# Eight routed experts on one core: ranking the experts, stacking a small expert's row parts, and splitting weights 2048 columns at a time

## The chip, the core and the metric

The kernel runs on one core of a Trainium2 chip. The metric is the device time of one execution in microseconds; a run gives the median over executions. The engines are TensorE (PE in the rows, its weight loads PEld), VectorE (DVE), ScalarE (ACT), GpSimd (POOL) and SyncE (SP), which here issues the DMA loads. They have queues of their own, work through them in order, and meet only at semaphores.

## The reference

All values are float32. The input is 256 tokens of width 1024. A first block of two layers mixes tokens and ends each layer with a feed-forward part. In the second layer this part is a mixture of eight experts:

```python
logits = (xt @ router)                       # 256 x 8
top_logit, top_e = lax.top_k(logits, 2)      # two experts for each token
gates = jax.nn.softmax(top_logit, axis=-1)
# each expert e, on the tokens that chose it (hidden width 3584):
yb = (jax.nn.silu(h @ w_gate[e]) * (h @ w_up[e])) @ w_down[e]
y = sum over a token's two experts of gate * yb
```

So 512 rows in all go to eight experts, and every expert's three matrices (1024 x 3584, 1024 x 3584 and 3584 x 1024) are read once. A second block of two layers follows, with attention, gating, a short convolution and a feed-forward part of width 2816.

## The kernel before

**Float32 in parts.** TensorE multiplies in a reduced form of float32. To keep the precision, `split` writes each operand as a high part H (a rounding copy on ScalarE, line 182) and a low part L = source - H (on VectorE, line 183). A product is three matmuls: H by H, L by H and H by L. For weights, `raw` (line 193) issues the load of 1 MB (128 partitions of 2048 columns) on SyncE into one of five buffers `wr`, and `parts` splits it in two halves of 1024 columns, into five buffers each of `wh` and `wl`.

**Routing.** `moe` computes logits, picks two experts per token by comparing all pairs, counts earlier tokens of the same expert with a triangular matmul, and so gives each row a slot `pos` in its expert. `one_hot` turns slots into a 0/1 matrix `oh`, with which TensorE gathers the rows of two experts at once, 128 slots each, into `xH` and `xL`. An expert with over 128 rows would set `over`, and `overflow` (a branch on that value ahead of the third expert) would work on the remaining rows.

**Experts.** They run one after the other in the order of their number, two to a gather. For each, a loop runs over seven blocks of 512 hidden columns. `gate_up` loads two 1 MB pieces each of the gate and up matrices, and multiplies the gathered rows (stationary, 128 x 128) with 512 weight columns (moving): 8 row blocks x 3 products x 2 matrices = 48 matmuls. ScalarE and VectorE make silu(gate) * up. `down`, always one block behind, transposes the result by four TensorE transposes (line 158), splits it into `aH` and `aL`, and adds 24 matmuls to the two output banks `py`. When an expert is done, its output is scaled by the gates (`y`), and `back` returns it to the tokens through the transposed one-hot `ohT` and adds it to `moe_out`.

**What sets the order.** The instructions are put in order by a planner when the program is built, by its own estimates of when each is ready; on each engine that order is then fixed. Loads are kept in the order of their use. Five early loads are placed in buffers that the stage uses only later (`places`), so that they can be issued ahead of the stage.

**After the experts.** The second block uses the same `wr`, `wh` and `wl` buffers through `cols`, `fm2` and `down`. In its feed-forward layer a 1 MB piece makes 48 matmuls of 256 columns, after which VectorE scales the result (line 1592) and does the short convolution (`conv3`, lines 1637 to 1639).

## Time and profile before

| | |
|---|---|
| median of 3 runs | 2883.36 us (2870.65 to 2900.98) |
| the profiled execution | 2886.99 us, of which the span 2885.2 us |
| granted TensorE clock, mean | 0.965 of full speed |
| TensorE / VectorE / ScalarE / GpSimd busy | 2750.6 / 1988.4 / 1468.3 / 348.5 us |
| loaded and stored by DMA | 585.8 MB, 203 GB/s over the span |
| loads of expert weights | 3 x 112 of 1024 KB |

The span is the time from the first to the last instruction. A busy share is a mean over stages that differ, so rows of single stages count for more. A row such as `L154 PE MATMUL psmoe<-wl,xH` names the line, the engine, the operation, and the tile written and the tiles read. Matmuls overlap in the array, so the time of one (some 0.40 us for 512 columns) is longer than the step from one to the next. An arrow in a row points to what the engine waited for. PEclk is the granted TensorE clock, DMA share the busy share of the 16 DMA engines.

### The profile page before, as it was taken

Reading aid. Unit: us, or ns where it says so; the run is one execution under the profiler, and the core shown is the slowest. Engines: PE = TensorE matmul, PEld = TensorE weight load, DVE = VectorE, ACT = ScalarE, POOL = GpSimd, SP = SyncE. Lnnn points to the kernel's source line nnn. Section 1 sums busy time; section 2 is a strip of 40 time slices with the busy share of each in tenths; the row PEclk is TensorE's granted clock in tenths of the full one; section 3 lists DMA queues with packets and bytes.
Section 4 is the critical chain, followed back from the end, with each engine's and each line's share of the span. In section 5 each row is a group of like instructions: output and inputs, shape, how many; then the busy total and the mean of one; then the engine's idle time right before and its main releaser. Section 6 shows DMA issues by size and latency. Waiting matters only on the chain. (4 is left out here: it accounts for less than half of the span.)

```text
span 2885.2 us, 42860 instructions
## 1 busy us (share of the span) xinstructions
PE 2750.6 (95%) x17006; PEld 2257.8 (78%) x17006; DVE 1988.4 (69%) x2753; ACT 1468.3 (51%) x2032; POOL 348.5 (12%) x256
## 2 busy tenths in 40 slices
PE   6998999999998879999989999999999999999999
PEld 4677656778886766677867777778777889998999
DVE  4685474322225796488878888888889868856784
ACT  3313243322224332477757777767777646644563
POOL 1420012211001610100000000000000221301120
PEclk9898799999999998999999999999999999999999
DMA  6122155333333224579988999899989835553453
GB/s 227 51 74 74 52 150 193 96 123 94 97 99 105 81 88 140 173 293 352 319 321 325 322 353 344 328 338 362 337 325 349 307 114 175 183 183 117 161 184 109
DMA packets 108098, 585.77 MB, mean 203 GB/s; under 512 B 12657, under 2 KB 19825, under 8 KB 54129
## 3 DMA queue, kind: packets, MB, share of 16 engines
q1 hardware_dynamic: 107888, 582.95, 57.5%
q8 instruction: 136, 2.23, 0.3%
q14 instruction: 74, 0.60, 0.1%
HBM read 580.80 MB, written 2.10 MB: 202 GB/s over the span
## 5 line engine op out<-in xcount | busy, mean ns | idle before, releaser
L183 DVE TENSOR_TENSOR wl<-wr,wh 128x1024 fp32r<-128x1024 f32 x978 | 1169.5, 1225 | 477.9 <-ACT wh L182 465.6
L182 ACT CAST wh<-wr 128x1024 fp32r<-128x1024 f32 x992 | 1003.8, 1044 | 681.1 <-PE psffn L154 193.2
L154 PE MATMUL psmoe<-wh,xH 128*128 128x512 f32 x896 | 354.9, 397 | 3.4 <-ACT wh L182 3.4
L154 PE MATMUL psmoe<-wl,xH 128*128 128x512 f32 x896 | 356.2, 398 | 1.0 <-DVE wl L183 0.7
L154 PE MATMUL psmoe<-wh,xL 128*128 128x512 f32 x896 | 355.5, 397 | 0.0
L154 PEld LDWEIGHTS psmoe<-wl,xH 128*128 128x128 f32 x896 | 168.3, 188 | 45.6 <-DVE wl L183 6.5
L154 PEld LDWEIGHTS psmoe<-wh,xH 128*128 128x128 f32 x896 | 168.4, 188 | 44.4 <-ACT wh L182 5.0
L154 PE MATMUL pssf<-oh,wl 128*128 128x256 f32 x704 | 199.5, 284 | 0.0
L154 PE MATMUL pssf<-ohT,wh 128*128 128x256 f32 x704 | 199.2, 284 | 0.0
L154 PEld LDWEIGHTS psmoe<-wh,xL 128*128 128x128 f32 x896 | 168.4, 188 | 39.1
L154 PE MATMUL pssf<-oh,wh 128*128 128x256 f32 x704 | 198.9, 284 | 0.0
L154 PE MATMUL psmoe<-wh,aL 128*128 128x512 f32 x448 | 178.3, 398 | 2.0 <-DVE aL L183 2.0
L154 PE MATMUL psmoe<-wh,aH 128*128 128x512 f32 x448 | 175.6, 397 | 2.5 <-ACT aH L182 2.5
L154 PE MATMUL psmoe<-wl,aH 128*128 128x512 f32 x448 | 163.3, 400 | 0.0
L1551 POOL TENSOR_SCALAR x<-x,fin 128x256 f32<-128x256 f32 x8 | 12.2, 1542 | 1057.5 <-DMA wr<-w_in 1057.3
L154 PE MATMUL psffn<-h2L,wh 128*128 128x512 f32 x352 | 138.7, 394 | 1.3 <-POOL h2L L257 1.3
L154 PE MATMUL psffn<-h2H,wh 128*128 128x512 f32 x352 | 138.2, 395 | 1.0 <-ACT h2H L256 1.0
L154 PE MATMUL psffn<-h2H,wl 128*128 128x512 f32 x352 | 137.5, 392 | 0.0
L154 PEld LDWEIGHTS pssf<-oh,wl 128*128 128x128 f32 x704 | 135.2, 192 | 0.0
L154 PEld LDWEIGHTS pssf<-ohT,wh 128*128 128x128 f32 x704 | 135.1, 192 | 0.0
L154 PEld LDWEIGHTS pssf<-oh,wh 128*128 128x128 f32 x704 | 135.0, 192 | 0.0
L154 PEld LDWEIGHTS psmoe<-wh,aL 128*128 128x128 f32 x448 | 84.2, 188 | 24.4 <-DVE aL L183 4.4
(476 smaller groups left out, 5624.6 us busy)
## 6 DMA issues: line engine op xcount, KB each, us to landing
wr<-moe_w_gate SPq DMA_DIRECT2D x112, 1024.0 KB, 7.0
wr<-moe_w_up SPq DMA_DIRECT2D x112, 1024.0 KB, 6.6
wr<-moe_w_down SPq DMA_DIRECT2D x112, 1024.0 KB, 7.0
wm<-mod_w SPq DMA_DIRECT2D x96, 512.0 KB, 4.3
wr<-f_up SPq DMA_DIRECT2D x44, 1024.0 KB, 4.9
wr<-w_in SPq DMA_DIRECT2D x52, 512.0 KB, 3.8
wr<-w_in SPq DMA_DIRECT2D x16, 1024.0 KB, 5.0
wr<-f_down SPq DMA_DIRECT2D x16, 1024.0 KB, 5.0
```

The costliest lines, as they stand in the source:

```text
L154: i = self.nc.tensor.matmul(out, lhsT, rhs, start=start, stop=stop, **kw)
L182: self.nc.scalar.copy(H, src)
L183: (eng or self.nc.vector).tensor_sub(L, src, H.bitcast(F32))
L1551: nc.gpsimd.tensor_scalar(x[:, k], x[:, k], fin[:, k:k + 1], None, op0=ALU.mult)
```

## The change

**Ranking.** VectorE counts the rows of each expert and ranks experts 1 to 7 by that count, largest first; expert 0 always keeps rank 0. Slots, one-hots and gates are from then on by rank. SyncE reads the expert numbers of ranks 1 to 7 into registers, and loads of their weights go to an address taken from such a register.

**Large and small.** Ranks 5, 6 and 7 are small: up to 64 rows. A small expert's one-hot has its 64 slots twice, and the gather puts the high part into the first 64 columns of the stationary operand and the low part into the other 64. Two products, by the weights' H and by their L, then stand for three. The two halves of the result are copied to SBUF and added in the matmul that turns them: its moving operand `fold` is two identity matrices on top of one another. The hidden values are split again into the two halves of one operand for `down`. `overflow` works on rows over 64 for these ranks.

**Order.** The groups are ranks (0, 5), (1, 6), (2, 7) and (3, 4). In the first three a block of the large expert and one of the small one take turns (the first group starts with two blocks of rank 0); in the last the two large experts follow each other. The overflow branch stands ahead of the second group. PSUM has two banks for gate and up in place of four, and four for the outputs in place of two.

**Splits.** From the experts on, and in the second block too, `parts` splits 2048 columns at once. There are three `wh` buffers and two `wl` buffers of that size; during the experts a third `wl` buffer lies in the stage's own pool. Four early loads have a place, where there were five.

```diff
@@ constants, parts, build
+SMALL = 5
...
-        n = max(1, 1024 // nf)
+        n = max(1, self.wide // nf)
         for k in range(0, nk, n):
             m = min(n, nk - k)
             H = self.wh.tile([128, m, nf], F32R, tag="wh", name=self.nm("wh"))
-            L = self.wl.tile([128, m, nf], F32R, tag="wl", name=self.nm("wl"))
+            self.nl = (self.nl + 1) % 3
+            wl = self.wl3 if self.wl3 and self.nl == 2 else self.wl
+            L = wl.tile([128, m, nf], F32R, tag="wl", name=self.nm("wl"), **({"bufs": 1} if wl is self.wl3 else {}))
...
+        self.wide = 1024
...
-                self.big = [wr2, big("wh2"), big("wl2")]
+                self.big = [wr2, big("wh2", 3), big("wl2", 2)]
...
         self.wr, self.wh, self.wl = self.big
+        self.wide = 2048
@@ moe: ranking
+                nc.vector.tensor_copy(cnt, pp[:, 2])
+                nc.vector.tensor_copy(key, cnt)
+                nc.vector.memset(key[:, 0:1], 1024.0)
+                i8 = self.iota[:, 0:8]
+                sq8, lt2 = [128, 8, 8], lt[:, 0]
+                a, c = key[:, None, :].to_broadcast(sq8), key[:, :, None].to_broadcast(sq8)
+                kg, ke = gt[:, 0], eq[:, 0]
+                nc.vector.tensor_tensor(kg, a, c, ALU.is_gt)
+                nc.vector.tensor_tensor(ke, a, c, ALU.is_equal)
+                nc.vector.tensor_tensor(ke, ke, lt2, ALU.mult)
+                nc.vector.tensor_add(kg, kg, ke)
+                rank = pr.tile([128, 8], F32, name="rank")
+                nc.vector.tensor_reduce(rank[:, :, None], kg, AX.X, ALU.add)
+                nc.vector.tensor_tensor(pm, rank[:, None, :].to_broadcast(sq8), i8[:, :, None].to_broadcast(sq8), ALU.is_equal)
+                def placed(o, v):
+                    for tt in range(2):
+                        w = pr.tile(sq8, F32, tag="plw", name=self.nm("plw"), bufs=2)
+                        nc.vector.tensor_tensor(w, pm, v[:, tt, None, :].to_broadcast(sq8), ALU.mult)
+                        nc.vector.tensor_reduce(o[:, tt, :, None], w, AX.X, ALU.add)
+                nc.vector.tensor_tensor(off, pp[:, 0:2], off, ALU.add)
+                placed(pos, off)
...
-                self.one_hot(oh, pos, 0, 0)
+                self.one_hot(oh, pos, 0, 0, 1)
+                self.one_hot_small(oh, pos, SMALL)
...
+                placed(ix, w)
+                nc.vector.tensor_copy(who, ix[:, 0])
+                nc.vector.tensor_scalar(w[:, 0], i8, SMALL - 0.5, 64.0, op0=ALU.is_gt, op1=ALU.mult)
+                nc.vector.tensor_add(w[:, 0], w[:, 0], ix[:, 1])
+                nc.vector.tensor_reduce(mx[:, 0], w[:, 0], AX.X, ALU.max)
@@ moe: experts
-            self.banks(ax="01", st="1", pp="2345", py="67")
+            self.banks(ax="01", st="1", pp="23", py="4567")
...
-                more = [(pg, "xH"), (pg, "xL"), (pe, "out"), (pe, "ohT"), (pg, "y")]
-                order = (6, 8, 10, 12, 14)
+                more = [(pg, "xH"), (pe, "out"), (pe, "ohT"), (pg, "y")]
+                order = (6, 8, 10, 12)
+                self.wl3 = pg
...
+                self.at = lambda n, j: A[n][0] if j == 0 else A[n][bass.ds(self.place[j], 1)][0]
...
                             ch = self.wload(w[fb, :, kh * 4:kh * 4 + 4], 4, 512)
-                            for i, (H, L) in enumerate(ch):
-                                k0 = kh * 4 + i * 2
-                                self.projT(ps, H, L, xh, xl, [(k, k0 + k) for k in range(2)], slice(0, 128), k0 == 0, k0 == 6)
+                            for H, L in ch:
+                                k0 = kh * 4
+                                if e < SMALL:
+                                    self.projT(ps, H, L, xh, xl, [(k, k0 + k) for k in range(4)], slice(0, 128), k0 == 0, k0 == 4)
+                                    continue
+                                for k in range(4):
+                                    self.mm(ps, xh[:, k0 + k], H[:, k], k0 + k == 0, False, chain=ps)
+                                    self.mm(ps, xh[:, k0 + k], L[:, k], False, k0 + k == 7, chain=ps)
...
+                    s = pg.tile([128, 2, 512], F32, tag="gu", name=self.nm("gu"), bufs=1)
+                    for i, ps in enumerate(pp):
+                        nc.scalar.copy(s[:, i], ps)
...
+                        pt = self.ps((128, 2, 4, 64))
+                        for i in range(2):
+                            for k in range(4):
+                                self.mm(pt[:, i, k], s[:, i, k * 128:(k + 1) * 128], fold, True, True, chain=pt)
+                        sT = pg.tile([128, 4, 64], F32, tag="s", name=self.nm("sT"))
+                        nc.scalar.activation(sT, pt[:, 0], AF.Silu)
+                        nc.vector.tensor_mul(sT, sT, pt[:, 1])
+                        aL = aH[:, :, 64:128]
+                        self.split(aH[:, :, 0:64], aL, sT)
...
+                        (H, L), = self.wload(self.at("moe_w_down", e)[2 * fb + kh], 2, 1024)
+                        for k in range(2):
...
+                                self.mm(py[o], aH[:, kh * 2 + k], H[:, k, c], first, False, chain=py[o])
+                                if n == 128:
+                                    self.mm(py[o], aL[:, kh * 2 + k], H[:, k, c], False, False, chain=py[o])
+                                self.mm(py[o], aH[:, kh * 2 + k], L[:, k, c], False, last, chain=py[o])
...
+                def gather(a, b, tag):
+                    H = pg.tile([128, 8, 2, 128], F32R, tag="xH", name=self.nm("xH"))
+                    L = pg.tile([128, 8, 128], F32R, tag="xL", name=self.nm("xL"))
+                    n = 1 if b is None else 2
+                    two = lambda t: t.rearrange("p a s -> p (a s)")
+                    for k in range(KT):
+                        ps = self.ps((128, 2, n, 128), tag=tag)
+                        for i, src in enumerate((hmH, hmL)):
+                            for tt in range(2):
+                                self.mm(two(ps[:, i]), src[:, tt, k * 128:(k + 1) * 128], oh[:, tt, a] if b is None else oh[:, tt, a:b + 1:b - a],
+                                        tt == 0, tt == 1, chain=ps)
+                        nc.scalar.copy(two(H[:, k])[:, 0:n * 128 - 64 * (n - 1)], two(ps[:, 0])[:, 0:n * 128 - 64 * (n - 1)])
+                        nc.vector.tensor_copy(L[:, k], ps[:, 1, 0])
+                        if b is not None:
+                            nc.vector.tensor_copy(H[:, k, 1, 64:128], ps[:, 1, 1, 64:128])
+                            xs[b] = H[:, :, 1], None
+                    xs[a] = H[:, :, 0], L
...
+                groups = [(0, 5), (1, 6), (2, 7), (3, 4)]
+                LAST = 4
+                units = [(0, 0), (0, 1)]
+                for fb in range(FB):
+                    units += [(SMALL, fb)] + [(0, fb + 2)] * (fb + 2 < FB)
+                for a, b in groups[1:3]:
+                    units += [(e, fb) for fb in range(FB) for e in (a, b)]
+                units += [(e, fb) for e in groups[3] for fb in range(FB)]
+                out = ohT = ahead = gate = None
+                waiting = []
+                def flush(n):
+                    while len(waiting) > n:
+                        e, fb, s = waiting.pop(0)
+                        if fb == 0:
+                            py[e] = [self.ps(tag="py") for _ in range(2)]
+                        down(e, fb, s, py[e])
+                        if fb == FB - 1:
+                            y = finish(e)
+                    return y if n == 0 and e == LAST else None
+                for n, (e, fb) in enumerate(units):
+                    if fb == 0:
+                        for a, b in groups:
+                            if e == a:
+                                if a == 1:
+                                    flush(0)
+                                    self.behind = None
+                                    self.overflow(out, hmH, hmL, oh, ohT, gs, pos, wt, most, pg)
+                                if a:
+                                    self.one_hot(oh, pos, a, 0, 1 if b >= SMALL else 2)
+                                    if b >= SMALL:
+                                        self.one_hot_small(oh, pos, b)
+                                gather(a, b if b >= SMALL else None, "ax" if a else "py")
+                        if e == LAST:
+                            gather(e, None, "ax")
+                        if e == SMALL:
+                            self.place = [None] + [nc.values_load(who[0:1, j:j + 1], engines=(mybir.EngineType.SP,), min_val=0, max_val=7) for j in range(1, E)]
+                            most = nc.values_load(over[0:1, 0:1], min_val=0, max_val=320)
+                    waiting.append((e, fb, gate_up(e, fb, *xs[e])))
+                    flush(1)
+                yH, yL = flush(0)
@@ helpers
...
+    def one_hot_small(self, oh, pos, e):
+        w = [128, 2, 2, 64]
+        self.nc.vector.tensor_tensor(oh[:, :, e].rearrange("p t (d s) -> p t d s", d=2), self.iota[:, None, None, 0:64].to_broadcast(w),
+                                     pos[:, :, e:e + 1, None].to_broadcast(w), ALU.is_equal)
...
```

## Rows read from the trace of the kernel before

**Rows 1.** The page: span; busy time, share, instructions by engine.

```profile
span 2885.2 us, 42860 instructions
PE 2750.6 (95%) x17006; PEld 2257.8 (78%) x17006; DVE 1988.4 (69%) x2753; ACT 1468.3 (51%) x2032; POOL 348.5 (12%) x256
```

**Rows 2.** Busy time by window: a steady unit, a boundary; columns in line one.

```profile
core 0: us, PE busy (x) PEld busy (x) DVE busy (x) ACT busy (x) POOL busy (x), PEclk, DMA share, GB/s
1708.24:1725.48 17.24, 17.24 (x78) 13.92 (x77) 15.00 (x15) 12.56 (x15) 0.00 (x0) 1.00 0.96 371
...
1759.96:1777.20 17.24, 14.76 (x78) 11.64 (x77) 15.11 (x21) 10.58 (x16) 0.00 (x0) 1.00 0.84 286
```

**Rows 3.** Chain of waits, expert stage: start us, us, what.

```profile
1773.05 24.86 PE psmoe L154 x117
...
1964.84 16.80 PE psmoe L154 x72
1982.08 16.80 PE psmoe L154 x72
...
2032.58 24.86 PE psmoe L154 x117
```

**Rows 4.** Waits, load queue, 1691 to 1757 us: total us, times, longest.

```profile
SPq L193 <- DVE wl L183: 57.3, 23, 3.6
```

**Rows 5.** Instructions grouped, 1262 to 2293 us: busy, mean ns, idle before.

```profile
L183 DVE TENSOR_TENSOR wl<-wr,wh 128x1024 fp32r<-128x1024 f32 x660 | 778.0, 1220 | 92.4 <-ACT wh L182 83.6 <-PE psmoe L154 4.1
L182 ACT CAST wh<-wr 128x1024 fp32r<-128x1024 f32 x660 | 662.1, 1050 | 84.3 <-PE psmoe L154 81.9 <-ACT wh L182 0.6 <-DVE wl L183 0.3
...
L1172 DVE TENSOR_TENSOR s<-s,psmoe 128x512 f32<-128x512 f32 x55 | 37.7, 685 | 24.3 <-PE psmoe L154 24.3
...
L1206 DVE CAST xL<-psmoe 128x256 fp32r<-128x256 f32 x24 | 9.2, 420 | 1.2 <-ACT xH L1205 1.1
```

**Rows 6.** Timeline, second block: start us, us, engine, line, operation.

```profile
2348.19 1.11 PE L154 MATMUL pssat<-vt,PT 128*128 128x64 f32 x8
```

**Rows 7.** Busy time by window of 5 us, columns as in Rows 2.

```profile
1260.00:1265.00 5.00, 5.00 (x23) 4.00 (x23) 5.00 (x7) 4.88 (x7) 0.00 (x0) 1.00 1.01 426
...
1565.00:1570.00 5.00, 5.00 (x23) 4.03 (x22) 4.47 (x4) 3.98 (x5) 0.00 (x0) 1.00 0.99 374
```

**Rows 8.** Groups of instructions, VectorE, routing, 1226 to 1262 us.

```profile
L1114 DVE TENSOR_TENSOR gt<-lg 128x128 f32<-128x128 f32 x1 | 0.3, 280 | 0.0
...
L1130 DVE TENSOR_TENSOR pos<-psrout,off 128x16 f32<-128x16 f32 x1 | 0.2, 175 | 0.6 <-PE psrout L154 0.6
```

**Rows 9.** Timeline of the load queue at the start of the experts.

```profile
1254.08 0.33 SPq L193 DMA_DIRECT2D wr<-moe_w_gate  x1
```

**Rows 10.** Timeline, second group: in brackets the idle time before.

```profile
1509.92 0.77 PE L154 MATMUL psmoe<-oh,hmH 128*128 128x256 f32 x2 [9.62 <-DVE oh L1275]
```

**Rows 11.** Timeline, TensorE, second block: neighbours of 128 and of 256 columns.

```profile
2300.34 0.28 PE L154 MATMUL pssp<-wh,hmH 128*128 128x128 f32 x1
2300.45 0.28 PE L154 MATMUL pssp<-wh,hmL 128*128 128x128 f32 x1
...
2305.09 0.28 PE L154 MATMUL pssp<-hmH,wh 128*128 128x256 f32 x1
2305.21 0.28 PE L154 MATMUL pssp<-hmL,wh 128*128 128x256 f32 x1
```

**Rows 12.** Chain of waits, second block's feed-forward layer.

```profile
2409.55 178.36 PE pssf L154 x1498
```

**Rows 13.** Groups of instructions, VectorE, second block, 2400 to 2590 us.

```profile
L183 DVE TENSOR_TENSOR wl<-wr,wh 128x1024 fp32r<-128x1024 f32 x65 | 82.3, 1266 | 31.6 <-ACT wh L182 31.0
...
L1638 DVE SCALAR_TENSOR_TENSOR moe_out<-u,prs,moe_out 128x255 f32<-128x255 f32 x44 | 28.1, 680 | 0.2
...
L1639 DVE SCALAR_TENSOR_TENSOR moe_out<-u,prs,moe_out 128x255 f32<-128x255 f32 x44 | 20.4, 499 | 0.0
...
L1592 DVE TENSOR_TENSOR u<-pssf,b 128x512 f32<-128x512 f32 x22 | 15.0, 680 | 0.0
```

More of the change, by code (lines that the diff above doesn't have):

```diff
@@ L323, in build @@
         self.nload, self.places = 0, {}
+        self.nl, self.wl3 = 0, None
+        self.wide = 1024
         self.leng = nc.vector
@@ L1090, in moe @@
             over = pe.tile([128, 1], I32, name="over")
+            who = pe.tile([128, 8], I32, name="who")
+            pm = pe.tile([128, 8, 8], F32, name="pm")
+            fold = pe.tile([128, 64], F32, name="fold")
+            nc.vector.tensor_add(fold, self.ident[:, 0:64], self.ident[:, 64:128])
             self.lab = "rout"
@@ L1129, in moe @@
                 nc.vector.tensor_scalar(off, sel, -4096.0, 4096.0, op0=ALU.mult, op1=ALU.add)
-                nc.vector.tensor_tensor(pos, pp[:, 0:2], off, ALU.add)
+                cnt = pr.tile([128, 8], F32, name="cnt")
+                key = pr.tile([128, 8], F32, name="key")
+                nc.vector.tensor_copy(cnt, pp[:, 2])
[19 more added lines that the diff above has]
+                placed(pos, off)
                 pts = []
@@ new lines, in gate_up @@
+                        pp.append(ps)
+                    if e < SMALL:
+                        s = pg.tile([128, 512], F32, tag="s", name=self.nm("s"))
+                        nc.scalar.activation(s, pp[0], AF.Silu)
+                        nc.vector.tensor_mul(s, s, pp[1])
+                        return s
+                    s = pg.tile([128, 2, 512], F32, tag="gu", name=self.nm("gu"), bufs=1)
+                    for i, ps in enumerate(pp):
+                        nc.scalar.copy(s[:, i], ps)
@@ L1173, in gate_up @@
                     return s
                 def down(e, fb, s, py):
-                    pt = self.ps((128, 4, 128))
-                    for k in range(4):
-                        self.tp(pt[:, k], s[:, k * 128:(k + 1) * 128], self.ident, chain=pt)
+                    n = 128 if e < SMALL else 64
                     aH = pg.tile([128, 4, 128], F32R, tag="aH", name=self.nm("aH"))
-                    aL = pg.tile([128, 4, 128], F32R, tag="aL", name=self.nm("aL"))
-                    self.split(aH, aL, pt)
+                    if e < SMALL:
+                        pt = self.ps((128, 4, 128))
+                        for k in range(4):
+                            self.tp(pt[:, k], s[:, k * 128:(k + 1) * 128], self.ident, chain=pt)
+                        aL = pg.tile([128, 4, 128], F32R, tag="aL", name=self.nm("aL"))
+                        self.split(aH, aL, pt)
+                    else:
+                        pt = self.ps((128, 2, 4, 64))
+                        for i in range(2):
+                            for k in range(4):
+                                self.mm(pt[:, i, k], s[:, i, k * 128:(k + 1) * 128], fold, True, True, chain=pt)
[4 more added lines that the diff above has]
+                        self.split(aH[:, :, 0:64], aL, sT)
@@ L1182, in down @@
+                    last_fb = FE // 512 - 1
                     for kh in range(2):
-                        for k, (H, L) in enumerate(self.wload(A["moe_w_down"][e, 2 * fb + kh], 2, 1024)):
-                            first, last = fb == 0 and kh == 0 and k == 0, fb == FE // 512 - 1 and kh == 1 and k == 1
+                        (H, L), = self.wload(self.at("moe_w_down", e)[2 * fb + kh], 2, 1024)
+                        for k in range(2):
+                            first, last = fb == 0 and kh == 0 and k == 0, fb == last_fb and kh == 1 and k == 1
@@ L1218, in moe, with finish @@
+                def finish(e):
+                    nonlocal out, ohT, ahead, gate
                     if e == 0:
@@ new lines, in finish @@
+                        nc.vector.scalar_tensor_tensor(yL[:, c], py[e][o], gs[:, e:e + 1], yH[:, c].bitcast(F32), op0=ALU.mult, op1=ALU.subtract)
+                    if e == LAST:
+                        return yH, yL
+                    for f, ps in self.back(e, yH, yL, ohT):
+                        if e == 0:
+                            nc.vector.tensor_copy(out[:, f:f + 2], ps)
+                        else:
+                            nc.vector.tensor_add(out[:, f:f + 2], out[:, f:f + 2], ps)
@@ L1255, in moe @@
                 begin, end = next(ahead)
-                for f, ps in self.back(E - 1, yH, yL, ohT):
+                for f, ps in self.back(LAST, yH, yL, ohT):
                     for j in range(2):
@@ L1297, in overflow @@
         with tc.If(over > 128):
-            w_ = lambda i: pg.tile([128, 8, 2, 128], F32R, tag=("xH", "xL")[i], name=self.nm("wo")).bitcast(F32).rearrange("p a b c -> p (a b c)")
+            w_ = lambda i: pg.tile([128, 8, 2, 128], F32R, tag="xH", name=self.nm("wo")).bitcast(F32).rearrange("p a b c -> p (a b c)")
+            for e in range(E):
+                self.one_hot(oh, pos, e, 128 if e < SMALL else 64, 1)
             for e in range(0, E, 2):
-                self.one_hot(oh, pos, e, 128)
-                self.slots(oh, ohT, gs, wt, e)
+                self.slots(oh, ohT, gs, wt, e, e + 1)
             f = lambda t: t.bitcast(F32)
@@ L1314, in overflow @@
                     pp = []
-                    for w in (A["moe_w_gate"][e], A["moe_w_up"][e]):
+                    for w in (self.at("moe_w_gate", e), self.at("moe_w_up", e)):
                         ps = self.ps(tag="pp")
```

94 lines of the change are left out of this document (33 added, 61 removed).

## The prediction

> **What bounds the kernel now.** The page first: TensorE is busy 95% of a span of 2885.2 us [rows 1], and the profiled execution as a whole took 2887.0 us, 3.6 above the 2883.4 median of the runs shown. That share is a mean, so I went to the stage the change touches, the eight experts, which runs from the first row gather at about 1241 us to about 2292. The windows are cut to one step of the loop (512 hidden columns of one expert, called a unit here). In a steady unit TensorE is busy 17.24 of 17.24 us, VectorE 15.0, ScalarE 12.6, and the DMA engines 96% at 371 GB/s [rows 2]: TensorE bounds it, with two others close behind. The chain of waits says the same: 72 matmuls in 16.80 us, 0.233 us each, and the next unit starts 17.24 us later [rows 3]; the missing 0.44 us are four transposes. The queue of loads waits only for VectorE to free a buffer, 23 times in 66 us [rows 4], so transfers are kept back and not late. Two experts make a group. The same piece of the chain comes back after 2032.58 - 1773.05 = 259.5 us [rows 3], of which 14 units are 241.4; the other 18.1 us go to gathering rows, scaling and returning results, and waits around them. A window across such a boundary shows TensorE at 14.8 of 17.2 us [rows 2].
>
> **The change part by part.**
>
> *Two passes in place of three for three experts.* Experts 5, 6 and 7 in rank drop 24 of 72 matmuls per unit: 48 x 0.233 = 11.2 us. Their folding adds eight fp32 matmuls of 64 columns; the nearest row is eight of just that shape in 1.11 us [rows 6]. A small unit is then 12.3 us of TensorE, and a pair (large and small) 29.5 where it was 34.5. Taken alone this is worth 7 x 5.0 = 35 us a group, 104 us in three.
>
> *What comes to the front instead.* A pair still loads 12 x 1.049 = 12.6 MB. The rows give two speeds for engines that are all busy: 374 GB/s in the middle of a group, 426 just after the stage's start, when many loads are queued [rows 7]. A pair costs 33.6 us by the first and 29.5 by the second. With TensorE no longer the limit the queue will be fuller than in mid-group, yet five buffers, some held by the splits, are less than the start had. I take the middle, 400 GB/s: 31.5 us a pair. VectorE: a split of 1024 columns takes 1.22 us and an operation of half that width 0.69 [rows 5], so 2048 columns take 1.22 + 2 x 0.53 = 2.28; twelve are 27.4 us, plus 1.4 for the large unit's two operations and 0.8 for the small one's (0.42 each for 256 columns) [rows 5]: 29.6. ScalarE, at 1.05 us per 1024 columns, is at most 25.2 for the splits and some 3 for the rest, and stays behind the three. So three limits lie between 29.5 and 31.5, and the highest decides.
>
> The page "DMA: Bandwidth & Descriptors" of the Trainium skill, section "Where 436 GB/s comes from", says that for loads from HBM a limit of about 358 GB/s per core binds. The windows of this trace at 371 and 426 GB/s are above it, so the trace does not agree for one core alone; by that rule a pair would be an estimated 35.1 us, and the change would gain nothing.
>
> *A group then.* Seven pairs are 220.5 us. Of the 18.1 us of boundary I keep 13, since TensorE has 2 us of room per pair but buffers reach only some loads ahead: 233.5, or 26 less than 259.5. For the second and third groups this makes **-52 us**.
>
> *The first group* keeps its full stop before the overflow test, where TensorE waits 9.6 us for the new one-hot [rows 10]; nothing here changes it. New is that SyncE must read the ranks into registers before it can issue the load of any expert but the first. Twelve loads of the first expert stand ahead of that and hold two units of work, 34 us, so TensorE is covered. Loads that were issued at 1254 [rows 9] move back by the reading of eight values, which no row shows: nothing if it is ready early, 10 us by the stop above. I take 6 us off this group's gain: **-20 us**. Register arithmetic for an address on each later load costs SyncE nothing that counts, because it issues one load in about 2.6 us. The extra places for early loads fall from five to four; within the same 6 us.
>
> *The last group* holds two large experts (ranks 3 and 4), stays at 17.24 us a unit, and gathers for each by itself: 64 matmuls of 128 columns at 0.112 us, against 32 of 256 at 0.12 [rows 11]: 7.2 - 3.8 = **+3.4 us**.
>
> *Ranking.* Thirteen more small VectorE operations stand before the first one-hot, and nine after it while VectorE is full. Rows of their kind take 0.175 to 0.28 us [rows 8]: 22 x 0.19 = **+4 us** (2 if half lie beside other work, 6 at the longer row).
>
> *Wide splits after the experts.* The second block, too, now splits 2048 columns at once, with two low-part buffers of that size (five of 1024 before) and three high-part ones. There TensorE runs 178 us without a gap [rows 12]; 1498 matmuls in that time are 0.119 us each, so a chunk of 48 is 5.7. When TensorE leaves a chunk, VectorE has until it finishes the next, 5.7 us, to do 0.68 (scaling), four conv operations and one split. By the means of its rows that is 0.68 + 2 x 0.68 + 2 x 0.50 + 2.28 = 5.3 [rows 13]. It fits, so I cost it at nothing: the cover is the chunk in the other buffer.
>
> *PSUM.* Gate and up have two banks in place of four. A bank is wanted again only after up and down of another unit (at least 3.7 us), while its reader takes 0.69 us [rows 5]. Nothing.
>
> Sum: -52 - 20 + 3.4 + 4 = -64.6; 2887.0 - 64.6 = 2822. Against the median it is 2819 to 2822; I state **2822**.
>
> **The rivals.**
>
> *Transfers bind at the mid-group speed.* For it: the DMA engines were 99% busy at 374 GB/s with VectorE and TensorE at work [rows 7]. Then a pair is 33.6 us, a group 235 + 13 = 248, 11 less than now: -22 - 7 + 7.4 = -22, **2865**. Against it: 426 in a window with TensorE full [rows 7]. By the Trainium skill's limit above, the pair would be longer still and the time that of before.
>
> *The compute engines stay the limit.* If the queue reaches 426, VectorE's 29.6 is the highest of three limits that all but meet, and a group takes 7 x 29.6 + 13 = 220, 39 less than now: -78 - 33 + 7 = -104, **2783**. For it: the same window at the start. Against: it leaves no room for any order that is not perfect.
>
> *Slower: the two low-part buffers starve the second block.* If the order written for VectorE puts the scaling and conv work of two chunks ahead of the next split, its turn is 2 x 3.04 + 2.28 = 8.4 us against 5.7 per chunk [rows 13]: 2.7 us lost on each. Over 44 up chunks (22 in each of two layers) that is 119 us: **2941**. It decides from the point where VectorE's turn exceeds 5.7 us, and outweighs the gain from 1.5 us per chunk. For it: the sum above that just fits. Against: TensorE never waits there now, and split work that is ready can be placed before conv work that waits for ScalarE.
>
> *The change doesn't do what it says:* if a small expert held over 64 rows, or a large one over 128, the overflow branch would load every expert again, over 800 us. Counting the reference's own routing of the given input, the experts get 66, 72, 53, 98, 54, 53, 64 and 52 rows; the three smallest are 53, 53 and 52. So it stays untaken.
>
> **How the numbers follow.** Forecast 0.55 (2795 to 2850), transfers at mid-group speed 0.21, compute still the limit 0.13, starved second block 0.10, overflow 0.01. About 1% is what a measurement of this kernel can tell from no change, which puts the bounds at 2855 and 2912. Faster: 0.55 of the forecast and 0.13 make 0.68; within 1%: the mid-group rival, 0.21; slower: 0.11. The range reaches down to 2785, about the price of the second rival, and up to 2880, past the first rival's 2865 with the doubts on ranks and ranking (10 + 6 us) at their far ends; outside remain the slower cases and what of the second rival goes below its price.
>
> **What would show it.** The matmul rows with the expert's input low part fall from 896 to 560, those with the hidden low part from 448 to 280. In the chain of waits, a pair of units should stand at 30 to 32 us, and the same piece should return after some 233 us; in windows of the second and third groups the DMA share should be about 1.0 at 395 to 426 GB/s with TensorE below full. If the share is 1.0 at 375, the first rival holds. If it is below 0.95 with TensorE idle, waits between engines took the gain, and the rows that end TensorE's idle time name them. The second block's chain should again show 1498 matmuls in one piece of 178 us; pieces of 48 with gaps before them would show the starved buffers. TensorE's restart after the overflow test should again be about 10 us. The prediction is wrong as a whole if the units of the last, unpaired group leave 17.24 us, since then the wide splits themselves changed the pace.

## The result and the profile after

The changed kernel takes 2966.6 us (median; 2963.3 to 2968.3) against 2889.0 for the kernel before, run beside it: a ratio of 1.0273, 95% interval 1.0214 to 1.0332. It is slower where 2822 us was forecast. Its profiled execution took 2968.3 us. The page's first rows, in answer to [rows 1]:

```profile
span 2966.4 us, 41670 instructions
PE 2713.3 (91%) x16786; PEld 2210.9 (75%) x16786; DVE 1949.2 (66%) x2387; ACT 1419.9 (48%) x1652; POOL 341.7 (12%) x256
```

TensorE has 220 matmuls less and 37 us less to do, and yet the span is 81 us longer. The stages, worked out from the traces, say where. A group runs from its first copy of gathered rows (`xH`) to the next group's, the last one to the experts' last matmul; the tail is the rest of the span. All in us, other kernels are told of below:

| kernel | groups 1, 2, 3 | last group | tail | median, ratio to before (95%) |
|---|---|---|---|---|
| before | 268.9, 260.6, 259.5 | 253.0 | 600.9 | 2889.0 |
| after | 270.8, 276.8, 277.3 | 285.8 | 612.0 | 2966.6, 1.027 (1.021 to 1.033) |
| narrow55 | 246.9, 238.3, 242.1 | 270.5 | 598.3 | 2838.3, 0.983 (0.980 to 0.985) |
| half | 247.8, 238.8, 245.4 | 265.1 | 607.2 | 2853.1, 0.990 (0.987 to 0.994) |
| smallhalf | 245.3, 236.6, 240.7 | 286.3 | 611.0 | 2871.2, 0.995 (0.993 to 0.997) |
| latecopy | 266.0, 254.9, 264.1 | 285.2 | 612.0 | 2928.2, 1.015 (1.013 to 1.018) |
| three | 269.3, 251.9, 265.7 | 286.6 | 612.0 | 2936.0, 1.015 (1.012 to 1.019) |
| three55 | 262.3, 246.6, 256.3 | 269.6 | 598.6 | 2887.4, 1.001 (0.999 to 1.004) |
| bwide32 | 271.4, 270.5, 264.6 | 257.2 | 611.6 | 2929.7, 1.014 (1.009 to 1.020) |
| joint55 | 246.4, 238.3, 242.2 | 257.4 | 604.3 | 2839.4, 0.986 (0.980 to 0.991) |
| mix2 | 245.0, 237.7, 242.4 | 257.7 | 606.3 | 2830.4, 0.980 (0.976 to 0.984) |

So nearly all of the loss lies in the experts (+68.7 us, of which the last group has 32.8), the rest in the tail (+11.1). The experts as a whole, before and after (columns as in [rows 2]):

```profile
1242.20:2284.30 1042.10, 1016.04 (x4540) 813.64 (x4539) 896.73 (x880) 748.23 (x833) 0.00 (x0) 0.99 0.91 336
1243.90:2354.44 1110.54, 981.53 (x4318) 768.77 (x4317) 856.98 (x579) 717.04 (x547) 0.00 (x0) 0.96 0.85 315
```

TensorE stands idle for 129.0 us of them, where it was 26.1, and its granted clock is lower. A steady pair of units and two units of the last group, by windows:

```profile
1592.16:1628.95 36.79, 31.83 (x141) 24.23 (x141) 28.91 (x17) 24.90 (x19) 0.00 (x0) 1.00 0.92 338
2115.07:2151.72 36.65, 34.60 (x152) 27.83 (x152) 31.31 (x17) 25.12 (x17) 0.00 (x0) 1.00 0.96 366
```

No engine and no transfer fills the pair: TensorE 31.8 of 36.8 us, VectorE 28.9, ScalarE 24.9, DMA 0.92. Such a row means that the engines wait for each other in turn. (The next pair takes 38.2 us; the mean is 37.5, where before two units took 34.5.) And the two large units of the unpaired group take 36.7 and not 34.5. The chain of waits through a small unit shows the turns (start us, us, what):

```profile
1610.80 0.02 ACT aH L183
...
1611.28 1.92 ACT wh L183
...
1613.21 2.30 DVE wl L184
...
1615.56 1.90 PE psmoe L155 x7
...
1617.48 0.02 ACT gu L1232
...
1617.96 1.91 ACT wh L183
...
1619.90 2.30 DVE wl L184
...
1622.25 1.91 PE psmoe L155 x7
...
1624.18 0.02 ACT gu L1232
...
1624.66 1.91 ACT wh L183
...
1626.60 2.30 DVE wl L184
...
1628.95 5.12 PE psmoe L155 x21
```

Read it as a circle of 6.7 us that comes round for each matrix: an operation of ScalarE that waits for TensorE (the copy `gu` or the cast `aH`) stands ahead of the cast of a weight piece; behind it comes that cast, 1.9 us, then VectorE's part of the split, 2.3 us, and only then can TensorE go on, for 1.9 us. The next pair is longer by TensorE's clock: there the matmuls at the same place of the circle take 3.33 us in place of 1.90.

```profile
1615.56:1617.46 1.90, 1.90 (x8) 1.43 (x8) 1.90 (x1) 0.00 (x0) 0.00 (x0) 1.00 0.61 129
1652.34:1655.67 3.33, 3.33 (x8) 2.44 (x8) 2.15 (x1) 0.00 (x0) 0.00 (x0) 0.51 0.88 285
```

The granted clock (PEclk) is 0.51 of full speed there, the lower of TensorE's two levels (1.2 and 2.4 GHz) for nearly the whole stretch. TensorE had waited 1.82 us for VectorE just before, but so it had in the first pair, where the clock stayed at 1.00; why the next one is hit is not shown. The waits from 1592 to 1705 us name the same three pairs of engines:

```profile
DVE wl L184 <- ACT wh L183: 23.5, 13, 3.6
ACT gu L1232 <- PE psmoe L155: 16.5, 6, 3.9
PEld psmoe L155 <- DVE wl L184: 15.0, 13, 2.1
ACT aH L183 <- PE psmoe L159: 11.1, 3, 3.7
```

Before, TensorE was busy in every part of a unit [rows 2]. The wide splits of the experts, 1262 to 2354 us, in answer to [rows 5]:

```profile
L184 DVE TENSOR_TENSOR wl<-wr,wh 128x2048 fp32r<-128x2048 f32 x330 | 746.2, 2288 | 203.6 <-ACT wh L183 195.9 <-PE psmoe L155 6.1
L183 ACT CAST wh<-wr 128x2048 fp32r<-128x2048 f32 x329 | 621.1, 1910 | 145.4 <-PE psmoe L155 133.8 <-issue 7.2 <-ACT wh L183 2.4
```

VectorE waits 195.9 us for casts ahead of its splits, where it was 83.6.

The tail, before and after:

```profile
2284.30:2885.20 600.90, 592.71 (x4823) 576.52 (x4822) 432.43 (x650) 314.16 (x494) 124.18 (x87) 0.99 0.46 154
2354.44:2966.40 611.96, 598.60 (x4825) 582.68 (x4824) 426.47 (x558) 296.18 (x402) 117.52 (x87) 0.97 0.44 150
```

Its 11.1 us are 5.2 more of idle time on TensorE and 5.9 that nearly the same matmuls take longer at a lower clock: from 2444 to 2459 us, say, it stood at 0.55, after 10 us in which TensorE was busy for 7.4. The chain of waits leads into the second block by another way, through GpSimd's norm, and has TensorE's next piece 18.8 us after the experts, where it was 9.3. But that is not where the tail grows. TensorE works beside the norm, with the second block's first matmul (`pssp`) 8.9 us after the experts (8.1 before):

```profile
2363.36 0.58 PE L155 MATMUL pssp<-hmH,wh 128*128 128x256 f32 x1 [1.18 <-ACT wh L183]
```

And smallhalf, told of below, has 8.9 us in its chain there and a tail of 611.0 us. The feed-forward layer is as it was [rows 12]:

```profile
2488.41 176.97 PE pssf L155 x1504
```

### The profile page after: what moved, and what is told of

The parts are those of the page before. It is cut to its first block, busy times and chain, and to the rows that moved or that the text cites. A ratio compares the mean times of both kernels' runs of the same rounds, so it can differ in the third digit from the quotient of the medians.

```text
span 2966.4 us, 41670 instructions
## 1 busy us (share of the span) xinstructions
PE 2713.3 (91%) x16786; PEld 2210.9 (75%) x16786; DVE 1949.2 (66%) x2387; ACT 1419.9 (48%) x1652; POOL 341.7 (12%) x256
## 5 line engine op out<-in xcount | busy, mean ns | idle before, releaser
L184 DVE TENSOR_TENSOR wl<-wr,wh 128x2048 fp32r<-128x2048 f32 (+2 forms) x550 | 1121.9, 2056 | 560.6 <-ACT wh L183 499.7
L183 ACT CAST wh<-wr 128x2048 fp32r<-128x2048 f32 (+1 forms) x564 | 947.4, 1693 | 697.5 <-PE psffn L155 193.2
L155 PE MATMUL psmoe<-wl,xH 128*128 128x512 f32 x896 | 369.9, 413 | 62.2 <-DVE wl L184 60.7
L155 PE MATMUL psmoe<-wh,xH 128*128 128x512 f32 x896 | 363.4, 406 | 19.1 <-ACT wh L183 19.0
L155 PE MATMUL psmoe<-wh,xL 128*128 128x512 f32 x560 | 222.6, 398 | 0.0
L155 PE MATMUL psmoe<-wl,aH 128*128 128x512 f32 x448 | 173.7, 406 | 5.9 <-DVE wl L184 5.9
L155 PEld LDWEIGHTS psmoe<-wh,xL 128*128 128x128 f32 x560 | 106.8, 191 | 23.6
L155 PE MATMUL psmoe<-wh,aL 128*128 128x512 f32 x280 | 110.4, 395 | 1.0 <-DVE aL L184 1.0
L155 PEld LDWEIGHTS psmoe<-wl,aH 128*128 128x128 f32 x448 | 83.7, 192 | 28.9 <-DVE wl L184 12.3
```

The source lines that it names most:

```text
L155: i = self.nc.tensor.matmul(out, lhsT, rhs, start=start, stop=stop, **kw)
L183: self.nc.scalar.copy(H, src)
L184: (eng or self.nc.vector).tensor_sub(L, src, H.bitcast(F32))
```

## The experiments

Theory W: the wide splits set the pace. Theory T: the turns of large and small experts, with copies on ScalarE and two banks for gate and up, do. Later W was divided: H, the length of one operation; B, the number of buffers; O, the order on ScalarE.

**narrow55**, the change without wide splits:

```diff
-                self.big = [wr2, big("wh2", 3), big("wl2", 2)]
+                self.big = [wr2, big("wh2", 5), big("wl2", 5)]
...
-        self.wide = 2048
+        self.wide = 1024
...
-                self.wl3 = pg
...
```

> The changed kernel with one part undone: splits are 1024 columns again, with five high-part and five low-part buffers of that size and no third buffer in the stage's pool; ranks, small experts, turns and the two PSUM banks stay. Theory W (the wide splits: a piece of 2048 columns costs 1.9 us on ScalarE and then 2.3 us on VectorE before TensorE may finish it, and three pieces are too few to hide that behind an order that is fixed): the pair of units falls from 37.5 us to 31 to 33, the last group returns to about 17.3 to 17.6 us a unit, and the time to 2810 to 2870. Theory T (the turns of large and small experts, with the small expert's two ScalarE copies and only two PSUM banks for gate and up): the pair stays at 36 us or more, the last group gets fast, and the time stays above 2910.

2838.3 us: 128 below the change, and below the kernel before. The pair takes 32.9 us, with the DMA engines all but full:

```profile
1573.94:1606.87 32.93, 32.07 (x140) 24.04 (x140) 29.56 (x29) 25.80 (x31) 0.00 (x0) 1.00 0.97 384
```

W holds, T falls. The last group stays 17 us too long.

**bwide32**, the reverse: the kernel before with `self.wide = 2048`, three `wh` and two `wl`. (A third `wl` of that size, which the change has in the experts and bwide33 was to have, finds no room there: the stage's pool wants 52 KB a partition and 49.1 are left. So a part of what bwide32 loses may be the missing buffer's.)

> The kernel before with one thing changed: weights are split 2048 columns at a time, with three high-part and two low-part buffers of that size (experts and second block). Theory W (the width of the splits itself slows the hand-over between the engines): the chain of waits leaves 17.24 us per unit, 17.9 to 19 us each, and the time is 2950 to 3030 us (60 to 140 above before). Theory T (the turns of large and small experts, with their copies on ScalarE and two banks for gate and up, are at fault): units stay at 17.2 to 17.4 us and the time is within 15 us of before.

Neither: towards the end of a group units still return after 17.24 us as [rows 3] have it, but the time is 43 us longer than its neighbour's, 21.7 of it in the groups (the second and third above all) and 10.7 in the tail.

```profile
2257.54 16.80 PE psmoe L154 x72
...
2274.77 16.81 PE psmoe L154 x72
```

The other 10 lie before the first gather, where the two programs do the same; from 1150 to 1200 us the granted clock was 0.73 in this execution and 0.90 in that of before. In the groups TensorE covers a wide split with twelve matmuls to a piece, but not all that a wide split holds up: from 1600 to 1700 us it is busy for 95.0 of 100 us (before, 197.7 of 200 from 1540 us). There it waits above all for the low part of the hidden values, whose split stands behind a wide one on VectorE:

```profile
1628.36 2.28 DVE L183 TENSOR_TENSOR wl<-wr,wh 128x2048 fp32r<-128x2048 f32 x1
...
1631.30 0.50 PE L154 MATMUL psmoe<-wh,aL 128*128 128x512 f32 x1 [1.67 <-DVE aL L183]
```

So width costs up to 43 us alone (49 between three and three55, below) and 128 together with the small units.

**half**: the change with its buffers of 2048 columns, each filled by two operations.

```diff
-            self.split(H, L, w[:, k:k + m], self.leng)
+            q = max(1, 1024 // nf)
+            for j in range(0, m, q):
+                u = min(j + q, m)
+                self.split(H[:, j:u], L[:, j:u], w[:, k + j:k + u], self.leng)
```

> The changed kernel with its 2048-column buffers (three high, three low in the experts), but each piece split by two operations of 1024 columns on each of ScalarE and VectorE. Theory L (what hurts is how long one operation runs before TensorE may begin on its piece): the pair of units falls from 37.5 to 32.9-34 us and the time to 2835-2880 us. Theory B (what hurts is that buffers come free only in whole pieces of 2048 columns, three at a time): the pair stays at 36-38 us and the time at 2930-2980 us. In between, both have a share, to be read off as the part of the 128 us between 2967 and 2838.

2853.1 us, the pair 32.98: length has 114 of the 128 us, the number of buffers at most the rest. The experts' row shows in what form:

```profile
1243.60:2240.67 997.07, 960.75 (x4320) 746.20 (x4318) 873.11 (x913) 738.94 (x880) 0.00 (x0) 0.99 0.92 351
```

Against the change TensorE is idle for 92.7 us less (36.3 and not 129.0), and as many matmuls take 20.8 us less, at a granted clock of 0.99 and not 0.96. The chain runs once through VectorE where it ran three times round:

```profile
1609.40 27.07 PE psmoe L155 x119
...
1641.11 1.23 DVE wl L184
...
1642.38 1.63 PE psmoe L155 x5
```

**smallhalf**: half-width operations for the three small experts only.

```diff
+                    self.ow = 2048 if e < SMALL else 1024
...
```

> The changed kernel with its 2048-column buffers, in which only the pieces of the three small experts are split by two operations of 1024 columns each; the large experts and the second block keep one operation per 2048 columns. Theory H (the cost sits where a small unit's pieces pass from engine to engine): pair 33-34.5 us, last group as in the change (287 us), time 2865 to 2895 us. If the large units' splits hurt as much: pair 35-36 us, time 2900 to 2935 us.

2871.2 us, and the last group at 286.3: 95 of the 128 us belong to the small experts' pieces. The pair is shorter than expected, with the DMA engines full (407 GB/s in this one; 391 over the 160 us from 1550, which hold five):

```profile
1622.67:1654.81 32.14, 31.55 (x140) 24.13 (x140) 29.32 (x23) 25.47 (x25) 0.00 (x0) 1.00 1.01 407
```

ScalarE's order between the copies is that of the change; only its waits have shrunk from 2.5 us, in the brackets of these timeline rows:

```profile
1645.06 0.59 ACT L1236 COPY gu<-psmoe 128x512 f32<-128x512 f32 x1 [1.11 <-PE psmoe L155]
...
1650.04 0.59 ACT L1236 COPY gu<-psmoe 128x512 f32<-128x512 f32 x1 [0.70 <-PE psmoe L155]
```

**latecopy**: full width, but the copy of a small unit's sums is ordered behind both casts of the next matrix.

```diff
+        for c in list(self.late):
+            c[0] += 1
+            if c[0] == 2:
+                self.late.remove(c)
+                i = self.nc.scalar.copy(c[1], c[2])
+                self.tc.add_manual_dep(i.ins, self.cast, NOSYNC, reason="copy behind the next matrix' casts")
...
-                    for i, ps in enumerate(pp):
-                        nc.scalar.copy(s[:, i], ps)
```

> The changed kernel with its 2048-column operations; only the order on ScalarE is another: a small unit's copy of the gate sums (and likewise of the up sums) stands behind both casts of the next matrix and no longer between them. Theory O (the order is what hurts: the copy waits 2.5 us for TensorE, with a cast behind it that could run): the copies' wait moves off the loop, the pair falls from 37.5 to 33.5-36 us and the time to 2870-2935 us. Theory H (it is the length of the wide operations that makes TensorE, ScalarE and VectorE take turns; the copy only shows it, since the cast behind it would wait for a buffer that TensorE holds): pair 36.5-38 us, time within 20 us of 2967.

O's numbers: 2928.2 us, the pair 34.6 and 35.9. The order is a part of it, 38 of the 128 us. What is left hangs at the third such place, where `aH` still stands ahead of a cast:

```profile
1626.26 0.59 ACT L183 CAST aH<-psmoe 128x512 fp32r<-128x512 f32 x1 [3.70 <-PE psmoe L159]
1626.74 5.51 ACT L183 CAST wh<-wr 128x2048 fp32r<-128x2048 f32 x3
```

H as I had put it (the copy only shows it) is too strong. What fits both runs, though no run shows it by itself: each of three places in a pair puts one cast and one split into the chain, 1.92 + 2.30 us at full width and 1.05 + 1.22 at half. Three times the difference of 1.95 is 5.9 us; of these half gives back 4.5 (37.5 to 33.0) and smallhalf 5.4 (to 32.1), each with some 0.7 us of the clock's.

**three**: the change with three passes for all experts (the first of five such edits).

```diff
-                                if e < SMALL:
+                                if True:
...
```

> The changed kernel with three passes for all eight experts, so no folding and 5 us more TensorE work per pair; ranks, turns, wide splits and buffers as in the change. What it leaves out: a small expert's rows are multiplied with the low part of the large one's rows, so only its time counts. Theory H (a wide split hurts where TensorE's own work on a piece, 8 matmuls in 1.9 us, is shorter than the split's 1.9 on ScalarE and 2.3 on VectorE, so that each waits for the other in turn): with 12 matmuls, 2.8 us, per piece the pair falls from 37.5 to 34.5-36.6 us although it holds more work, and the time is 2915 to 2960 us. Theory S (each wide piece costs the same extra time whatever TensorE has to do): the pair rises to 40-43 us and the time to 3030-3090 us.

2936.0 us: 31 less than the change, with more matmuls to do. A pair takes 34.2 us (two units, below), TensorE without a gap. It agrees with H but doesn't prove it, since the copies of the sums fall away as well.

```profile
1601.17:1635.35 34.18, 34.18 (x153) 27.71 (x152) 29.34 (x17) 24.70 (x16) 0.00 (x0) 1.00 0.98 366
```

**three55**: the same in narrow55.

> The same three passes everywhere (the same low part used for both experts of a pair, so only the time counts) in the kernel with 1024-column splits and five buffers of each kind. It prices the two passes by themselves: TensorE has 34.5 us per pair, against a pair of 32.9 us with two passes. If the two passes are what that kernel gains by: pair 34.5-35.2 us, time 2870 to 2895 us. If its gain has another source (ranks, turns): within 10 us of 2838.

2887.4 us, no different from before: all that narrow55 gains, 49 us, comes from the two passes; ranks and turns by themselves bring nothing that can be told.

**joint55**: narrow55, with ranks 3 and 4 gathered together.

```diff
-                                gather(a, b if b >= SMALL else None, "ax" if a else "py")
-                        if e == LAST:
-                            gather(e, None, "ax")
+                                gather(a, b, "ax" if a else "py")
...
```

> The kernel with 1024-column splits and five buffers of each kind (2838 us) with one thing more: the last two large experts gather their rows in one go, 32 matmuls of 256 columns as before, in place of 64 of 128. In that kernel's chain TensorE stops for about 10 us at the second of the two gathers, and a restart of a few us follows. Theory G (the last group's extra 17 us are mostly that second stop): 2820 to 2830 us, last group 255 to 261 us. Theory Q (it is the queue of loads that arrives empty at the last group, or the two banks): within 5 us of 2838.

The last group falls to 257.4 us as G says, but the median stays at 2839.4, and the interval is too wide to tell 8 us. In the profiled execution 6 of the 13 us come back as a longer tail, and there the granted clock is the difference: after the experts it stands at 0.50 for 20 us here, and at 0.59 for 12 us in narrow55.

```profile
2235.00:2255.00 20.00, 19.86 (x94) 19.67 (x94) 10.86 (x19) 8.00 (x14) 10.49 (x10) 0.50 0.39 130
...
2248.00:2260.00 12.00, 11.86 (x65) 11.67 (x66) 8.03 (x14) 5.60 (x10) 10.04 (x8) 0.59 0.53 175
```

Nor are the 13 us all the second gather's: at the first one, from 1970 to 1980 us, narrow55 has a clock of 0.55 and joint55 one of 1.00, which is some 5 us. In narrow55's chain the second gather, which stands alone, is away from TensorE's matmuls of weights for 8.7 us:

```profile
2099.91 2.25 PE psmoe L155 x11
...
2110.82 5.34 PE psmoe L155 x22
```

**late1024**: the change, with pieces of 1024 columns from the second block on, in the same buffers.

> The changed kernel; only from the end of the experts on (second block) are weights split 1024 columns at a time, each piece in a buffer of the same 2048-column size (three high, two low). Theory W: the way from the last matmul of the experts to the second block's first long chain goes from 19 us back to 9-12, and the rest of the tail gains 1 to 4 us: 2950 to 2958 us. If that way is long for lack of buffers or from the order of the work, it stays 17-21 us and the time within 5 us of 2967.

The chain's way into the second block goes back to 9.3 us, as W says, but the time rises to 2991.6. With half the columns in three high and two low buffers, TensorE runs dry on each piece; the chain of its feed-forward layer:

```profile
2523.99 4.27 PE pssf L155 x34
...
2528.28 0.69 DVE u L1726
2528.97 1.14 DVE wl L184
...
2530.16 4.26 PE pssf L155 x34
```

What counts most here is how many columns the buffers hold: the tail is 598 to 606 us with five narrow buffers of each kind, 611 to 612 with three and two wide ones (607 in half, with half-width operations), 632 with three and two narrow ones. The steps of a few us among these are no larger than what the clock makes between narrow55 and joint55.

**pp3**: the change with three banks for gate and up, and one for transposes and gathers.

> The changed kernel with three PSUM banks for gate and up in place of two (one for the rest in place of two). If two banks are what holds TensorE, the pair falls by 2 us or more and the time by 40 us or more. By theory W it stays within 20 us of the changed kernel's 2967, or gets slower, since one bank is left for transposes, gathers and returns.

3042.1 us, 75 above the change; groups of 280.7, 283.5 and 293.2, the last 324. Its edit took a bank from the transposes and gathers, so the loss may be that bank's. The copies wait as before (17.6 us in six), so a third bank doesn't open the circle. Two banks against four was not tried alone.

**fine10**: joint55 with loads of 1024 columns into ten buffers.

> The kernel with 1024-column splits and a joint last gather (2839 us), with its loads cut in two: ten buffers of 1024 columns in place of five of 2048, each given back after one split. Theory D (transfers set the 32.9 us of a pair, and they run at 383 GB/s and not at the start's 426 because a load can only be issued when a whole buffer comes free): DMA above 390 GB/s, pair 31.9 to 32.4 us, time 2812 to 2830 us. If the speed of the transfers doesn't depend on how finely buffers come free: pair 32.7-33.2 us, time within 7 us of 2839; if smaller transfers are slower: pair above 33.5 us, time above 2850 us.

2860.7 us, the pair 34.2 at 373 GB/s: smaller transfers are slower, and D falls.

```profile
1593.28:1627.46 34.18, 32.78 (x141) 23.89 (x141) 29.55 (x29) 25.66 (x31) 0.00 (x0) 1.00 1.00 373
```

**mix2**: wide buffers in the experts, half-width operations for small units and the last group, joint gather, and five narrow buffers of each kind from the second block on.

> The best parts put together: buffers of 2048 columns in the experts, one operation of 2048 for the large experts of the pairs, two of 1024 for the small ones and for the last group, which gathers jointly; from the second block on 1024-column splits in five buffers of each kind. If the stages keep the lengths that they had apart (gathers at 1242 us, groups of 245, 237 and 241 us, a last group of 254 to 258, a tail of 598 to 602): 2816 to 2828 us, some 10 to 20 below the kernel with narrow splits throughout. Rival: the order planned for the tail again puts the first matmuls behind the norm (19 us in place of 9), or exchanging the buffers stops the engines: 2830 to 2850 us.

2830.4 us, 0.980 of before (0.976 to 0.984). The groups have the lengths expected; the tail is 606 and not 598 to 602, with the granted clock at 0.50 from 2230 to 2250 us, after the experts, as in joint55. It lies at the edge between the two forecasts, and is the lowest median of all, though its interval overlaps that of narrow55.

## Why the prediction was wrong

**The step that failed** is "So three limits lie between 29.5 and 31.5, and the highest decides." It counted a wide split by its busy time, and the busy times were right (2.30 us where I worked out 2.28; VectorE 28.9 us per pair where I had 29.6). But the three engines hand one piece to the next, and the order on each is fixed. What a wide split adds is the time until the next engine may begin, at every place where something that waits for TensorE stands ahead of a cast: three times 1.92 + 2.30 us in a pair's chain. So the pair took 37.5 us and not 31.5, and half-width operations in the same buffers gave 114 us back. I looked for this cover in the second block alone and never for the experts, though the small unit has only eight matmuls, 1.9 us, to hide a split of 2.3. The sign that I named for being wrong as a whole, units of the last group that leave 17.24 us, is what came. And TensorE's clock had no place in the sum: over the experts, where it now stood for 129 us, it was granted 0.96, where it had been 0.99.

**The pair without that.** Of the pace itself 31.5 us was nearly right: 32.1 in smallhalf (391 GB/s over five pairs) and 32.9 in narrow55 (384), where I took 400 GB/s. TensorE's term was too low as well. I priced the fold at eight rows of the trace; its eight float32 matmuls stand there as sixteen, two such rows in a small unit:

```profile
1618.12 1.10 PE L155 MATMUL psmoe<-fold,gu 128*128 128x64 f32 x8 [0.45 <-ACT gu L1232]
...
1624.90 1.03 PE L155 MATMUL psmoe<-fold,gu 128*128 128x64 f32 x8
```

That is 2.1 us and not 1.1. Whether transfers or TensorE (31.6 of 32.1 us busy in smallhalf) hold the pair, no run separates. Groups 2 and 3 without the wide splits are 238.3 and 242.1 us in narrow55 against 233.5 forecast: -40 and not -52.

**The first group** without them gains 22.0 us (246.9 against 268.9), where I had 20, and that is luck: the other groups gained 20 and not 26, and two things that I had wrong made up for it. I took 6 us off for reading the ranks, which no row of before showed. It keeps the load queue for some 4 us, and the next load is issued at 1251.5 (the load of [rows 9] was issued at 1254.1); operations grouped by the tile that they read, with shortest, middle and longest time in ns and the first and last start:

```profile
L1371 SPq TENSOR_LOAD <-who x7: 262/268/469, 1246.5 to 1250.2; - x7
```

TensorE's restart after the overflow test [rows 10] waits 5.2 us in the change and 6.2 in narrow55, where it was 9.6; I had said that nothing changes it:

```profile
1513.42 0.77 PE L155 MATMUL psmoe<-oh,hmH 128*128 128x256 f32 x2 [5.21 <-DVE oh L1406]
```

**The last group** was given +3.4 us, the difference of the gathers' matmuls. It is +17.5 in narrow55 and +4.4 in joint55: two gathers in place of one cost 13 us. At the second TensorE is away from the weights for 8.7 us, and at the first a lower clock takes some 5. In the change it is +32.8; half-width operations with the two gathers left as they are bring it to 265.1, so some 20 us are the wide splits'. Of these some 5 are the clock's (0.50 from 2068 to 2078 us, after the first gather) and the larger part idle time. Why they cost so much here and only 4 us in bwide32's last group (257.2), I have not settled; banks and order differ.

**Ranking**, at +4 us, can't be told: the first copy of gathered rows comes at 1242.2 us before and 1243.9 after, but kernels that do the same up to there have it at 1235.8 (three55) to 1252.3 (three).

**The second block** was right in its term (the layer took 178.36 us and takes 176.97), and my slower rival wrong for this change: its buffers do not starve. They do in late1024, which has the same number of half the size: 1.9 and 2.6 us lost at pieces by turns, where the rival had 2.7. What I did not foresee lies outside that layer: 5.2 us more of idle time and 5.9 of a lower clock in the tail.

**PSUM** was put at nothing, and the runs neither show nor exclude that. **The overflow branch** stayed untaken: the matmul rows with the low parts are the 560 and 280 forecast.

**The transfers.** The page "DMA: Bandwidth & Descriptors" of the Trainium skill, section "Where 436 GB/s comes from", by whose limit of about 358 GB/s the change could gain nothing, does not agree with the 391 GB/s of smallhalf's pairs, nor with narrow55's 384. The rival of transfers at mid-group speed had 33.6 us a pair, and narrow55's, at 32.9 with the DMA engines at 0.97, lie nearer to it than to the forecast; smallhalf's lie nearer to the forecast. (That rival's first group was added up wrongly: 11 less 6 is 5 us and not 7, and its time 2867.)

## What to carry over

Before the largest busy time is taken as the pace of several engines, ask of every operation that becomes longer which engine waits for its end, and with how much work in hand. A wider operation saves instructions and lengthens each hand-over; here it cost 43 to 49 us in all where the consumer's work on one piece was longer than the split (twelve matmuls, 2.8 us, against 2.3) and 128 us where three experts' was shorter (eight, 1.9 us). When a change has two halves, here fewer passes and wider splits, price them against each other: the first took away the cover that the second needed. And read the granted clock of a stage beside its busy times: 20.8 of the 113.5 us between the change and half in the experts are the clock's.

## What was not expected of the hardware

Loads of 1 MB ran at 391 GB/s over 160 us with TensorE, VectorE and ScalarE at work (smallhalf, DMA share 0.99), and loads of half that size at 369 over 170 us with the DMA engines equally full (fine10, 0.99): the share alone doesn't say which pace the transfers can keep.

Two programs can differ in TensorE's pace at the same granted clock of 1.00: 72 matmuls took 16.80 us in [rows 3] and in bwide32, but 16.52 in three55 and joint55. Why is not shown.

The times of one program's runs go with their granted clock: three55's span 2871.0 us, at a mean clock of 0.967, to 2899.7, at 0.956, and mix2's 2809.4 (0.968) to 2845.4 (0.956). So a difference of a few us between two kernels is not to be read from one profile of each.
